# State-space items re-spaced over later products, a reordered list of products, and ScalarE shifts in a two-block layer on one core

## Chip, cores and metric

One core of one Trainium2 chip runs the whole program. The metric is device microseconds (us) of one execution. Engines: TensorE (PE; its weight loads are PEld), VectorE (DVE), ScalarE (ACT), GpSimd (POOL), and SyncE (SP), whose queue issues most of the DMAs.

## The reference, cut to what matters

The input is one sequence of 256 rows of width 1024 in float32. A first block (two layers: modulated norms, pooling, sparse attention, feed-forward) is followed by a second block, and the change lies in the second block alone, apart from one buffer count. What the second block computes:

```python
u = h @ w_in
z, xbc, dt_f_raw, dt_b_raw, q, k, v, gate_logits = split(u)
y_ssd = ssd_branch(z, xbc, dt_f_raw, dt_b_raw, ...) @ w_proj_ssd
y_att = attention_branch(q, k, v) @ w_proj_attn
gates = sigmoid(gate_logits + b_gate)
mix = (gates[0] * y_ssd + gates[1] * y_att) @ w_out
h = layer_norm(alpha * h + mix)
h = layer_norm(alpha * h + square(relu(h @ w_up)) @ w_down)
# ssd_branch, forward and backward in time, by chunks of 128 rows:
xbc = silu(conv5(xbc))                       # xs (32 heads of 64), B, C (4 groups of 128)
lmat = exp(a_cs[l] - a_cs[s])  for s <= l    # running sums of dt * a, head by head
y = (C B^T * lmat) @ (dt * x) + what comes from the other chunk + d_skip * x
y = y * silu(z); y = y * rsqrt(mean(y^2 over a group)) * norm_w
```

## The kernel before

Every weight matrix is loaded in chunks of 128 x 1024 (`Weights.load`, lines 129 to 147): a DMA on SP's queue into `wst`, a copy on ScalarE that rounds it to `wh` (line 140), and a subtraction on VectorE that leaves the rest in `wl` (line 141). Each product is then three matmuls (line 89 in the trace, the helper `mm`). In the second block at most `cap=4` chunks are alive at once.

`large2` (line 1540) is a generator that runs the products in the order of `ORDER2`: v0, qk0 to qk2, v1, B, C, then x0 x1 z0 x2 z1 x3 z2 z3, then the gates g2 g3, pa (attention projection), g0 g1, and ps (state-space projection). Each of these takes 8 steps, pa 4 and ps 32: x0 runs over steps 56 to 63, the next seven over 64 to 119, g2 over 120 to 127, g3 to 135, pa to 139, g0 to 147, g1 to 155, ps over 156 to 187. An x product ends in a convolution (`conv`, lines 1319 to 1332): per half of its columns two scalings on ScalarE, eight VectorE instructions on line 1330, a tanh on ScalarE (line 1331) and a product on VectorE (line 1332). A z product ends in `zgate` (lines 1343, 1344).

Between the steps a `Plan` (lines 326 to 358) emits other work. Each entry has a step from which it may run and names of what it needs. The state-space work is 16 items, one for each group g (of 4), chunk t (of 2) and half of the group's heads (sub, of 2). Item i is placed at a = ss0 + ds * i, with ss0=73 and ds=4.2: steps 73 to 136. Its parts:
- `ssd_r` at a-6: two row loads on SP's queue (line 1421) into R, forward and backward running sums spread over all partitions
- `ssd_g` at a-3.5: four ScalarE scalings and four VectorE instructions (lines 1431, 1433)
- `ssd_d` at a: per head a ScalarE shift of the backward plane `u` (line 1443) and a VectorE instruction that subtracts the forward sum from `E` and takes the minimum with `u` (line 1444), then one exp (line 1445) and one product (line 1446)
- `ssd_y` at a+3.5: matmuls; for the second half of a pair also the sums (lines 1461 to 1467, one of them on GpSimd)
- `ssd_norm` at a+8 for the second half: product with z, square on ScalarE, power on GpSimd, scaling (lines 1472 to 1477)

`ssd_fm` (line 1481) of a group turns its two normed tiles y by TensorE transposes, scales them (line 1489) and splits them into high and low parts (lines 103, 106), which `proj_ssd` multiplies. Its step is a + sf with sf=300, past the end of the list, so it is emitted only when `proj_ssd` asks for it: `plan.until(("fm", k // 4))` ahead of chunk k = 0, 4, 8 and 12.

Work tiles are of one kind, `t2` (128 x 512 float32), with `nt2=22` buffers for the whole program. What is emitted earlier has the higher priority; the framework's scheduler may still put a later instruction ahead of one that, by its own reckoning, is not ready.

Of the kernel before, what the change touches and what calls it, by code (L numbers as in the profile page):

```python
# [11 lines left out]
AF = mybir.ActivationFunctionType  # L12
OP = mybir.AluOpType
# [11 lines left out]
ALPHA = 2.0 ** 0.25  # L25

SZ = 1024
TU = dict(nst=5, tabc=2, nw=9, nt2=22, raw=1, krest=2, qrest=4, pool2=1, c2=3, c3=1, c4=1, ln=3, uv='uv', pre=[1], nv=5, nv1=0, nv0=0, u0=19.5, du=0.7, ub=2, uc=4, c0=32.5, dc=0.1, w0=36, dw=0.5, comp=22, pool=27, dpool=2, cmpa=32, cmpb=34, dcmp=2, e1=1, e0=1, pta=2, ahead=3, modp=3, rf=0.95, r0=0, r0b=2, r1=0.8, r1b=1.2, rs=14, raw_=4, qrest_=6, u0_=19.5, du_=1.0, comp_=22, pool_=26, cmpa_=31, cmpb_=35, nv_=0, nv0_=0, w0_=32, dw_=0.8, order2='v0 qk0 qk1 qk2 v1 B C x0 x1 z0 x2 z1 x3 z2 z3 g2 g3 pa g0 g1 ps', dts=8, dcd=30, par0=10, par1=40, d0=50, dd=2, db=3, dc2=5, ss0=73, ds=4.2, scb=5, sx=3, sr=6, sg=3.5, sy=3.5, sn=8, sf=300, mf0=5, modp1=99, rf1=0.5, pool2_=3, c3_=2, c4_=3, nv1_=2, dpool_=2, dcmp_=1, dc_=0.4, cap=4, ub_=2.5, c0_=32.5, pta_=4)
NST, NW = TU['nst'], TU['nw']
NT2, NT4, NS5 = TU['nt2'], 5, 20  # L30

ORDER2 = TU["order2"].split()

MODS = {("mix", 0): ((0, 2), (0, 3), (0, 4)), ("ff", 0): [(0, 5), (1, 1), (1, 0), (1, 2), (1, 3), (1, 4)][:TU["mf0"]],
        ("mix", 1): [(0, 5), (1, 1), (1, 0), (1, 2), (1, 3), (1, 4)][TU["mf0"]:], ("ff", 1): ((1, 5),)}
CONV2 = {"x0": 0, "x1": 4, "x2": 8, "x3": 12, "B": 16, "C": 20}
# [23 lines left out]
def tile_two_blocks(ctx: ExitStack, tc: tile.TileContext, I, out, stop=None, dbg=None):  # L62
    nc = tc.nc
    V, A, G, T = nc.vector, nc.scalar, nc.gpsimd, nc.tensor
# [10 lines left out]
    def bank(tag):  # L75
        return pp.tile([128, 512], FT, name=tag, tag=tag, bufs={"acc": 4, "st": 2, "tr": 1, "pv": 1}[tag])
# [8 lines left out]
    def s5(shape, name, dt=FT):  # L85
        return small.tile(shape, dt, name=name, tag="s5", bufs=NS5)

    def mm(o, l, r, start, stop=False):
        T.matmul(o, l, r, start=start, stop=stop, skip_group_check=True)  # L89

    def fl(a):
        return a.rearrange("p a b -> p (a b)")
# [17 lines left out]
    def C(n):  # L110
        a, w = CC[n]
        return cst[:, a:a + w]
# [363 lines left out]
    for l in range(DEPTH):  # L476
        wi, wo = kt_view(I["w_in"][l]), kt_view(I["w_out"][l])
        g = {}
        cols = {"u": (0, 512), "q": (512, 1024), "k": (1024, 1536), "v": (1536, 1816)}
        if l == 0:  # L480
            for k in range(0, 8, 2):
                for n in "qk":
                    W.specs.append(([wi[:, k:k + 2, cols[n][0]:cols[n][1]]], 2, 512))
        for n in "qk" + TU["uv"]:
            if l or n in "uv":
# [6 lines left out]
    g2 = {}  # L492
# [715 lines left out]
    av, dt_, wo_, ed, sums = (s5([128, 2, 64], n) for n in ("av", "dt_", "wo_", "ed", "sums"))  # L1208
# [24 lines left out]
    def chunk_decays():  # L1233


        b = bank("st")
        for t in range(2):
            mm(b[0:32, t * 128:(t + 1) * 128], av[:, t, 0:32], C("j_le_l"), t == 0, True)
            mm(b[32:64, t * 128:(t + 1) * 128], av[:, t, 32:64], C("j_lt_s"), t == 0, True)
        rows = small.tile([64, 2, 128], FT, name="rows")  # L1240
        A.activation(fl(rows)[0:32], b[0:32, :256], AF.Copy)
        A.activation(fl(rows)[32:64], b[32:64, :256], AF.Copy, scale=-1.0)
        nc.scalar.dma_start(rows_d.rearrange("t h l -> h t l"), rows)
        b = bank("st")
        for t in range(2):
            T.transpose(b[:, t * 64:(t + 1) * 64], rows[:, t], ident[:64, :64])
        bv = b[:, :128].rearrange("p (t h) -> p t h", t=2)
        V.tensor_copy(sums[:, :, 0:32], bv[:, :, 0:32])
        V.tensor_scalar(sums[:, :, 32:64], bv[:, :, 32:64], -1.0, None, op0=OP.mult)
        b = bank("tr")  # L1250
        mm(b[:, 0:32], C("s_lt_j"), av[:, 0, :32], True, True)
        mm(b[:, 32:64], C("j_lt_s"), av[:, 1, 32:], False, True)
        mm(b[:, 64:96], C("j_ge_l"), av[:, 0, 32:], False, True)
        mm(b[:, 96:128], C("j_le_l"), av[:, 1, :32], False, True)
        A.activation(fl(ed), b[:, :128], AF.Exp)
        for t in range(2):
            V.scalar_tensor_tensor(wo_[:, t, :32], fl(ed)[:, t * 32:t * 32 + 32], 0.5, dt_[:, t, t * 32:t * 32 + 32], op0=OP.mult, op1=OP.mult)
# [178 lines left out]
    def ssd_d(g, t, sub):  # L1436


        a0 = g * 8 + sub * 4
        E, u = ssd.pop(("R", g, t, sub))  # L1440
        for i in range(4):
            h = a0 + i
            A.activation(u[:, i], u[:, i], AF.Identity, bias=sums[:, t, 32 + h:33 + h])
            V.scalar_tensor_tensor(E[:, i], E[:, i], sums[:, t, h:h + 1], u[:, i], op0=OP.subtract, op1=OP.min)  # L1444
        A.activation(fl(E), fl(E), AF.Exp)
        V.tensor_tensor(E, E, ssd.pop(("G", g, t, sub)), op=OP.mult)  # L1446
        ssd["M", g, t, sub] = E
# [111 lines left out]
    plan = Plan()  # L1559
    plan.at(TU["dts"], steps, needs=("v0",), gives="steps")  # L1560
    plan.at(TU["dcd"], chunk_decays, needs=("steps",), gives="decays")
    for i in range(2):
        plan.at(TU["par%d" % i], parity, i, needs=(f"v{i}",), gives=f"par{i}")
    for i in range(8):
        e, j = i // 4, i % 4
        a = TU["d0"] + TU["dd"] * i
# [6 lines left out]
    for i, it in enumerate(items):  # L1573
        g, t, sub = it
        a = TU["ss0"] + TU["ds"] * i
        if it[1:] == (0, 0):
            plan.at(a - TU["scb"], ssd_cb, g, needs=("B", "C", "steps"), gives=("cb", g))
            for tt in range(2):
                plan.at(a - TU["sx"] + 2 * tt, ssd_x, g, tt, needs=(f"x{g}", "decays"), gives=("x", g, tt))
        plan.at(a - TU["sr"], ssd_r, *it, needs=("decays", prev and ("r",) + prev), gives=("r",) + it)  # L1580
        plan.at(a - TU["sg"], ssd_g, *it, needs=(("cb", g),), gives=("g",) + it)
        plan.at(a, ssd_d, *it, needs=(("r",) + it, ("g",) + it), gives=("d",) + it)
        plan.at(a + TU["sy"], ssd_y, *it, needs=(("d",) + it, ("x", g, 0), ("x", g, 1), prev and ("y",) + prev), gives=("y",) + it)
        if sub:
            plan.at(a + TU["sn"], ssd_norm, g, t, needs=(("y",) + it, f"z{g}{t}"), gives=("n", g, t))
            if t:
                plan.at(a + TU["sf"], ssd_fm, g, needs=(("n", g, 0), ("n", g, 1)), gives=("fm", g))
        prev = it
    plan.got.add(None)
    plan.run(large2())  # L1590
# [170 lines left out]
```

## Time and profile before

| | us |
|---|---|
| median of 3 runs (1280.6 to 1288.57) | 1282.55 |
| the profiled execution: its time | 1284.53 |
| the profiled execution: its span | 1282.4 |
| TensorE busy | 1179.8 (92%) |
| VectorE busy | 895.9 (70%) |
| ScalarE busy | 642.4 (50%) |
| GpSimd busy | 237.0 (18%) |

The span runs from the first to the last instruction; the execution's time is 2.1 us longer. Times in the rows below count from the span's start. Matmuls are pipelined and their ends are modelled, so a busy TensorE may still be waiting for little things. An instruction's duration on VectorE and ScalarE is longer than the distance to the start of the next, because neighbours overlap a little.

### The profile page before, as it was taken

The page shows a single profiled execution, that of the slowest core. Times are in us where ns is not written, and L with a number is a line of the kernel's source. Part 1 is how long each engine was busy: PE and PEld are TensorE (multiplying, and loading weights), DVE is VectorE, ACT ScalarE, POOL GpSimd, SP SyncE. Part 2 cuts the span into 40 slices and gives each one's busy share as a digit, 9 for nine tenths or more (in the row PEclk, how much of TensorE's full clock was granted, in tenths as well). Part 3 has the DMA queues.
Part 4 walks back from the last instruction along what each step waited for, and adds up shares of the span by engine and source line. Part 5 has one row for each costly group of instructions (what it writes and reads, how often), then busy time and mean ns, then how long its engine had stood idle before and what let it go on. Part 6 is the DMA issues. An engine that isn't in the chain of part 4 may idle for free.

```text
span 1282.4 us, 19159 instructions
## 1 busy us (share of the span) xinstructions
PE 1179.8 (92%) x7188; PEld 1037.6 (81%) x7188; DVE 895.9 (70%) x1446; ACT 642.4 (50%) x1070; POOL 237.0 (18%) x233
## 2 busy tenths in 40 slices
PE   4878898999898899999999999988898899999997
PEld 3656776899787788789998999977688888799896
DVE  5777798887758768764545738799999557754544
ACT  4346355444535554744543545485675434544440
POOL 3553322112315101210100000011112001210101
PEclk9788889999999999999999999989899899999999
DMA  7855667889878534566663663564466753666640
GB/s 268 284 174 180 230 214 230 292 297 330 289 218 266 189 99 119 190 207 192 181 193 101 216 200 102 195 174 139 135 191 189 258 151 98 226 210 188 183 145 33
DMA packets 101780, 249.18 MB, mean 194 GB/s; under 512 B 9780, under 2 KB 15028, under 8 KB 101688
## 3 DMA queue, kind: packets, MB, share of 16 engines
q1 hardware_dynamic: 100904, 247.12, 60.6%
q8 instruction: 56, 0.92, 0.3%
q10 hardware_dynamic: 784, 0.85, 0.2%
q14 instruction: 36, 0.29, 0.1%
HBM read 246.03 MB, written 1.11 MB: 193 GB/s over the span
## 4 chain that ended last, share of the span: by engine, by line
PE 38%; issue 10%; DVE 8%; ACT 1%; POOL 1%; DMA 0%; DVEq 0%; POOLq 0%; ACTq 0%
PE acc L89 23%; PE st L89 12%; DVE wl L141 2%; DVE R L1444 1%; DVE cv L1330 1%; PE pv L89 1%; DVE G L1433 1%; DVE R L1446 1%; ACT wh L140 1%; POOL yss L119 0%; DVE ytmp L1465 0%; DMA wst<-in_w_up_dram 0%; PE tr L89 0%; POOL fr L380 0%; DVE yg L1477 0%
## 5 line engine op out<-in xcount | busy, mean ns | idle before, releaser
L141 DVE TENSOR_TENSOR wl<-wst,wh 128x1024 fp32r<-128x1024 f32 (+3 forms) x340 | 418.6, 1244 | 164.7 <-ACT wh L140 163.7
L140 ACT ACTIVATE wh<-wst 128x1024 fp32r<-128x1024 f32 (+3 forms) x340 | 352.1, 1048 | 314.2 <-PE acc L89 98.1
L89 PE MATMUL st<-hh,wh 128*128 128x256 f32 x576 | 163.0, 283 | 0.0
L89 PE MATMUL st<-hl,wh 128*128 128x256 f32 x576 | 163.0, 283 | 0.0
L89 PE MATMUL st<-hh,wl 128*128 128x256 f32 x576 | 163.0, 283 | 0.0
L89 PE MATMUL acc<-wh,frl 128*128 128x512 f32 x384 | 151.8, 395 | 2.4 <-DVE frl L381 2.3
L89 PE MATMUL acc<-wl,frh 128*128 128x512 f32 x384 | 150.6, 392 | 0.0
L89 PE MATMUL acc<-wh,frh 128*128 128x512 f32 x384 | 150.3, 391 | 0.0
L380 POOL TENSOR_TENSOR fr<-fr 128x512 f32<-128x512 f32 x48 | 64.7, 1349 | 384.7 <-ACT frh L379 376.4
L89 PE MATMUL acc<-hh,wl 128*128 128x256 f32 x416 | 122.1, 294 | 1.4 <-DVE wl L141 1.4
L89 PE MATMUL acc<-hl,wh 128*128 128x256 f32 x416 | 119.0, 286 | 0.0
L89 PE MATMUL acc<-hh,wh 128*128 128x256 f32 x416 | 118.7, 285 | 0.0
L89 PEld LDWEIGHTS st<-hh,wl 128*128 128x128 f32 x576 | 110.5, 192 | 0.7
L89 PEld LDWEIGHTS st<-hl,wh 128*128 128x128 f32 x576 | 110.5, 192 | 0.7
L89 PEld LDWEIGHTS st<-hh,wh 128*128 128x128 f32 x576 | 110.5, 192 | 0.0
L89 PE MATMUL acc<-wl,hh 128*128 128x512 f32 (+3 forms) x224 | 90.6, 405 | 13.1 <-DVE wl L141 13.1
L89 PE MATMUL acc<-wh,hl 128*128 128x512 f32 (+3 forms) x224 | 90.2, 413 | 12.4 <-ACT wh L140 9.9
L548 DVE SCALAR_TENSOR_TENSOR macc<-wst,cact,macc 128x1024 f32<-128x1024 f32 x70 | 91.7, 1311 | 7.5 <-DMA wst<-in_w_mod_dram 3.9
L89 PE MATMUL acc<-wh,hh 128*128 128x512 f32 (+3 forms) x224 | 90.6, 405 | 0.0
L89 PEld LDWEIGHTS acc<-wh,frl 128*128 128x128 f32 x384 | 72.6, 189 | 19.6 <-DVE frl L381 5.4
L89 PEld LDWEIGHTS acc<-wh,frh 128*128 128x128 f32 x384 | 72.5, 189 | 15.5
L89 PEld LDWEIGHTS acc<-wl,frh 128*128 128x128 f32 x384 | 72.5, 189 | 14.0
(328 smaller groups left out, 2289.6 us busy)
## 6 DMA issues: line engine op xcount, KB each, us to landing
wst<-in_w_ff_dram SPq DMA_DIRECT2D x128, 512.0 KB, 4.4
wst<-in_w_mod_dram SPq DMA_DIRECT2D x96, 512.0 KB, 4.6
wst<-in_w_in_dram SPq DMA_DIRECT2D x92, 512.0 KB, 4.8
wst<-in_w_up_dram SPq DMA_DIRECT2D x32, 512.0 KB, 4.3
wst<-in_w_down_dram SPq DMA_DIRECT2D x32, 512.0 KB, 4.3
wst<-in_w_out_dram SPq DMA_DIRECT2D x24, 512.0 KB, 4.2
R<-rows SPq DMA_DIRECT2D x32, 256.0 KB, 5.4
wst<-in_w_proj_ssd_dram SPq DMA_DIRECT2D x16, 512.0 KB, 4.7
```

Source lines behind the costliest of these rows:

```text
L89: T.matmul(o, l, r, start=start, stop=stop, skip_group_check=True)
L140: A.activation(h[:, :kc * n], st[:, :kc * n], AF.Copy)
L141: V.tensor_tensor(l[:, :kc * n], st[:, :kc * n], h[:, :kc * n], op=OP.subtract)
L380: G.tensor_tensor(r, r, r, op=OP.mult)
L548: V.scalar_tensor_tensor(acc, st, cact[:, k:k + 1], acc, op0=OP.mult, op1=OP.add)
L1330: V.scalar_tensor_tensor(v[:, a:e], u[:, a + j - 2:e + j - 2], w[:, j:j + 1], v[:, a:e], op0=OP.mult, op1=OP.add)
L1433: V.scalar_tensor_tensor(gm[:, i], cl, dt_[:, t, 32 + a0 + i:33 + a0 + i], gm[:, i], op0=OP.mult, op1=OP.add)
L1444: V.scalar_tensor_tensor(E[:, i], E[:, i], sums[:, t, h:h + 1], u[:, i], op0=OP.subtract, op1=OP.min)
L1446: V.tensor_tensor(E, E, ssd.pop(("G", g, t, sub)), op=OP.mult)
```

## The change

- `nt2` goes from 22 to 24.
- In `order2` the x and z products take turns: x0 z0 x1 z1 x2 z2 x3 z3.
- The items go to a = 70 + 5.6 * i: steps 70 to 154 (ss0=70, ds=5.6).
- `ssd_fm` of group g gets the step fm0 + dfm * g = 148 + 9 * g (148, 157, 166, 175); `sf` is gone.
- The column form of the running sums, `sums`, is negated for the forward half too, in one instruction in place of two.
- In `ssd_d` ScalarE adds the negated sum to the forward plane as well, and the four fused VectorE instructions of an item become one minimum over 128 x 512.

```diff
-TU = dict(nst=5, tabc=2, nw=9, nt2=22,
...
-order2='v0 qk0 qk1 qk2 v1 B C x0 x1 z0 x2 z1 x3 z2 z3 g2 g3 pa g0 g1 ps', dts=8,
...
-ss0=73, ds=4.2, scb=5, sx=3, sr=6, sg=3.5, sy=3.5, sn=8, sf=300,
+TU = dict(nst=5, tabc=2, nw=9, nt2=24,
...
+order2='v0 qk0 qk1 qk2 v1 B C x0 z0 x1 z1 x2 z2 x3 z3 g2 g3 pa g0 g1 ps', fm0=148, dfm=9, dts=8,
...
+ss0=70, ds=5.6, scb=5, sx=3, sr=6, sg=3.5, sy=3.5, sn=8,
...
-        V.tensor_copy(sums[:, :, 0:32], bv[:, :, 0:32])
-        V.tensor_scalar(sums[:, :, 32:64], bv[:, :, 32:64], -1.0, None, op0=OP.mult)
+        V.tensor_scalar(sums, bv, -1.0, None, op0=OP.mult)
...
         for i in range(4):
             h = a0 + i
+            A.activation(E[:, i], E[:, i], AF.Identity, bias=sums[:, t, h:h + 1])
             A.activation(u[:, i], u[:, i], AF.Identity, bias=sums[:, t, 32 + h:33 + h])
-            V.scalar_tensor_tensor(E[:, i], E[:, i], sums[:, t, h:h + 1], u[:, i], op0=OP.subtract, op1=OP.min)
+        V.tensor_tensor(E, E, u, op=OP.min)
         A.activation(fl(E), fl(E), AF.Exp)
...
-                plan.at(a + TU["sf"], ssd_fm, g, needs=(("n", g, 0), ("n", g, 1)), gives=("fm", g))
+                plan.at(TU["fm0"] + TU["dfm"] * g, ssd_fm, g, needs=(("n", g, 0), ("n", g, 1)), gives=("fm", g))
```

## Rows read from the trace of the kernel before

**Rows 1.** The page: busy time of each engine over the whole span.
```profile
PE 1179.8 (92%) x7188; PEld 1037.6 (81%) x7188; DVE 895.9 (70%) x1446; ACT 642.4 (50%) x1070; POOL 237.0 (18%) x233
```
**Rows 2.** Busy time by stretch: length, PE, PEld, DVE, ACT, POOL, PE clock, DMA share, GB/s.
```profile
830.00:993.00 163.00, 142.36 (x883) 123.48 (x882) 153.76 (x310) 112.06 (x235) 27.90 (x24) 0.93 0.57 165
993.00:1007.00 14.00, 14.00 (x120) 14.00 (x118) 9.84 (x9) 8.11 (x12) 0.00 (x0) 1.00 0.91 327
1007.00:1017.00 10.00, 6.58 (x35) 6.14 (x34) 6.49 (x13) 4.67 (x12) 0.00 (x0) 0.66 0.79 275
1017.00:1038.00 21.00, 21.00 (x178) 21.00 (x177) 8.58 (x7) 7.52 (x8) 0.00 (x0) 1.00 0.49 154
1038.00:1046.00 8.00, 5.24 (x43) 4.77 (x42) 6.49 (x13) 4.47 (x10) 0.00 (x0) 1.00 0.43 131
...
808.80:1007.00 198.20, 177.56 (x1159) 157.59 (x1158) 181.53 (x360) 129.30 (x269) 27.90 (x24) 0.94 0.59 175
```
**Rows 3.** The chain that ended last, 879 to 898: start, us, what.
```profile
883.37 1.22 DVE wl L141
...
886.92 1.05 DVE R L1444 x4
...
889.75 0.60 DVE R L1446
...
894.08 0.60 DVE yg L1461
894.68 0.60 DVE ytmp L1465
895.28 2.08 DVE R L1444 x4
```
**Rows 4.** Waits, 808 to 1007: who waited for whom, us in total, times, longest.
```profile
ACT R L1443 <- DMA R<-rows: 11.5, 8, 7.3
...
PE acc L89 <- ACT wh L140: 9.9, 2, 5.8
...
PE pv L89 <- DVE R L1446: 6.8, 8, 2.7
```
**Rows 5.** ScalarE in order of time: start, us, instruction, count, idle before it.
```profile
825.78 1.28 ACT L1443 ACTIVATE R<-R,sums 128x128 f32<-128x128 f32 x4 [7.27 <-DMA R<-rows]
826.97 1.26 ACT L1431 ACTIVATE G<-cbu,dt__6387 128x128 f32<-128x128 f32 x4
...
912.93 1.15 ACT L1331 ACTIVATE page<-cv 128x512 f32<-128x512 f32 x2 [2.56 <-DVE cv L1330]
913.98 4.83 ACT L140 ACTIVATE wh<-wst 128x1024 fp32r<-128x1024 f32 x5
```
**Rows 6.** TensorE in order of time, at the third convolution and in ps.
```profile
908.64 0.60 PE L1487 MATMUL st<-cst,yg 128*128 128x128 f32 x4
915.08 1.74 PE L89 MATMUL acc<-wh,hl 128*128 128x512 f32 x3 [5.83 <-ACT wh L140]
...
1007.00 0.60 PE L1487 MATMUL tr<-cst,yg 128*128 128x128 f32 x4
1008.38 0.65 PE L1487 MATMUL tr<-cst,yg 128*128 128x128 f32 x4 [0.79 <-DVE yw L1489]
1011.67 1.09 PE L1487 MATMUL st<-cst,yg 128*128 128x128 f32 x4 [2.63 <-DVE yw L1489]
```
**Rows 7.** VectorE in order of time: two transposed groups, ahead of ps's first matmuls.
```profile
1010.84 0.69 DVE L1489 TENSOR_TENSOR yw<-st,par 128x512 f32<-128x512 f32 x1
1011.44 0.68 DVE L1489 TENSOR_TENSOR yw<-tr,par 128x512 f32<-128x512 f32 x1
1012.04 1.42 DVE L106 TENSOR_TENSOR yl<-yw,yh 128x256 fp32r<-128x256 f32 x4
1013.37 0.69 DVE L1489 TENSOR_TENSOR yw<-st,par 128x512 f32<-128x512 f32 x1
```
**Rows 8.** SP's queue, whole span: what its DMAs waited for, us, times, longest.
```profile
SPq L135 <- DVE wl L141: 696.2, 262, 17.6
...
SPq L1421 <- DVE G L1433: 4.3, 1, 4.3
...
SPq L1421 <- ACT zs L1474: 2.8, 2, 1.6
...
SPq L702 <- DMA wst<-in_w_in_dram: 2.3, 2, 1.4
```

More of the change, by code (lines that the diff above doesn't have):

```diff
@@ L27 @@
 SZ = 1024
-TU = dict(nst=5, tabc=2, nw=9, nt2=22, raw=1, krest=2, qrest=4, pool2=1, c2=3, c3=1, c4=1, ln=3, uv='uv', pre=[1], nv=5, nv1=0, nv0=0, u0=19.5, du=0.7, ub=2, uc=4, c0=32.5, dc=0.1, w0=36, dw=0.5, comp=22, pool=27, dpool=2, cmpa=32, cmpb=34, dcmp=2, e1=1, e0=1, pta=2, ahead=3, modp=3, rf=0.95, r0=0, r0b=2, r1=0.8, r1b=1.2, rs=14, raw_=4, qrest_=6, u0_=19.5, du_=1.0, comp_=22, pool_=26, cmpa_=31, cmpb_=35, nv_=0, nv0_=0, w0_=32, dw_=0.8, order2='v0 qk0 qk1 qk2 v1 B C x0 x1 z0 x2 z1 x3 z2 z3 g2 g3 pa g0 g1 ps', dts=8, dcd=30, par0=10, par1=40, d0=50, dd=2, db=3, dc2=5, ss0=73, ds=4.2, scb=5, sx=3, sr=6, sg=3.5, sy=3.5, sn=8, sf=300, mf0=5, modp1=99, rf1=0.5, pool2_=3, c3_=2, c4_=3, nv1_=2, dpool_=2, dcmp_=1, dc_=0.4, cap=4, ub_=2.5, c0_=32.5, pta_=4)
+TU = dict(nst=5, tabc=2, nw=9, nt2=24, raw=1, krest=2, qrest=4, pool2=1, c2=3, c3=1, c4=1, ln=3, uv='uv', pre=[1], nv=5, nv1=0, nv0=0, u0=19.5, du=0.7, ub=2, uc=4, c0=32.5, dc=0.1, w0=36, dw=0.5, comp=22, pool=27, dpool=2, cmpa=32, cmpb=34, dcmp=2, e1=1, e0=1, pta=2, ahead=3, modp=3, rf=0.95, r0=0, r0b=2, r1=0.8, r1b=1.2, rs=14, raw_=4, qrest_=6, u0_=19.5, du_=1.0, comp_=22, pool_=26, cmpa_=31, cmpb_=35, nv_=0, nv0_=0, w0_=32, dw_=0.8, order2='v0 qk0 qk1 qk2 v1 B C x0 z0 x1 z1 x2 z2 x3 z3 g2 g3 pa g0 g1 ps', fm0=148, dfm=9, dts=8, dcd=30, par0=10, par1=40, d0=50, dd=2, db=3, dc2=5, ss0=70, ds=5.6, scb=5, sx=3, sr=6, sg=3.5, sy=3.5, sn=8, mf0=5, modp1=99, rf1=0.5, pool2_=3, c3_=2, c4_=3, nv1_=2, dpool_=2, dcmp_=1, dc_=0.4, cap=4, ub_=2.5, c0_=32.5, pta_=4)
 NST, NW = TU['nst'], TU['nw']
```

## Prediction

> **What bounds the kernel now.** I read the page first, then the chain that ended last, then busy time by stretch, then waits and timelines where the change touches. Over the whole span TensorE is busy 92% and VectorE 70% [rows 1], which suggests that work on VectorE is free. The stretch in question says otherwise. I cut it at 808.8, where ScalarE takes the first columns of x0 (step 63), and at 1007.0, where the last matmul of g1 gives way to ps's first transposes (step 156). In these 198.2 us VectorE is busy 181.5, TensorE 177.6 at a clock share of 0.94, ScalarE 129.3. From 830 to 993 VectorE is busy 153.8 of 163.0, that is 94.3%, and TensorE only 142.4, at 0.93; from 993 on VectorE has 9.8 of 14.0 and TensorE is full [rows 2]. So the items keep VectorE saturated until 993, the weight halves on line 141 come late, TensorE starves, and only then runs at its own pace. The chain says the same: around 890 it goes through VectorE instruction after instruction [rows 3].
>
> Two further losses matter. At 915.08 TensorE had waited 5.83 us for `wh`, because the copies of line 140 stood on ScalarE behind line 1331, which itself waited for the convolution on VectorE [rows 5, 6]. And ps begins with the transposes of `ssd_fm`: TensorE waits for VectorE's `yw` and for the halves [rows 6]. From 1017 to 1038 it does 178 matmuls in 21.0 us, 0.118 each. By that price the 35 from 1007 to 1017 need 4.1 of the 10.0 us (loss 5.9, with the clock share at 0.66), and the 43 from 1038 to 1046 need 5.1 of 8.0 (loss 2.9): together 8.8 us [rows 2]. The groups come in two bunches, not four, since the scheduler moves some of it ahead: the first transposes on bank `st` run at 908.64 [rows 6]. A step of the plan is thus a priority, not a time.
>
> **The change, part by part.**
>
> *Negated sums.* One VectorE instruction less, once, some sixty steps before it is used: nothing.
>
> *Minimum in one instruction.* VectorE loses 64 fused instructions: four take 1.05 us on the chain, or 2.08 right after `ytmp`, when GpSimd is adding [rows 3]. It gains 16 minima over 128 x 512; not in the trace, but the product of line 1446 has the same shape and operands and takes 0.60 [rows 3]. 16 x (1.05 - 0.60) = 7.2 us less work. The slow variant would make it 16 x 1.48 = 23.7, but it is a wait for GpSimd that the next instruction with two SBUF operands can inherit, so I take 7.2; 0 is the other end.
>
> *Shifts on ScalarE.* 64 more of a kind it already does. Four start at 825.78 and the next instruction at 826.97: 0.30 each, 19.0 us in all [rows 5]. ScalarE then has 129.3 + 19.0 = 148.3 in the stretch, against 198.2 - 129.3 = 68.9 us of idle time that covers it [rows 2]. I cost it at nothing on the path. If the cover fails, what is late is the `wh` copy queued behind the shifts, then `wl`, then TensorE: up to 19.0. An item also needs both R planes ahead of its first shift now; the wait on row loads is 11.5 us in 8 places [rows 4] and could at worst double.
>
> A rule of the Trainium skill speaks against this part: "ScalarE: Activation LUTs", Rules for kernel authors, wants add, multiply and the like on VectorE and not on ScalarE. By engine time the rows agree with it, since 19.0 us are paid for 7.2. By it the change would lose; that is the slower rival below.
>
> *Spreading the items.* Sixteen items over 84 steps in place of 63. Nothing is removed. Work moves from the saturated part into g0, g1 and the start of ps, where VectorE has room. Past step 156 go the last pair's sums and norm (0.60 + 0.60 [rows 3], and about as much for lines 1472 and 1477): 2.3 us. Into the stretch comes `ssd_fm` of group 0, two `yw` at 0.60 and four halves in 1.33: 2.5 us [rows 7]. VectorE's work in the stretch becomes 181.5 - 7.2 - 2.3 + 2.5 = 174.5.
>
> How fast can that be done? At a full VectorE, 174.5 us, 23.7 less than now. At the share it held while it had a backlog, 94.3%, 174.5 / 0.943 = 185.0: 13.2 less. At the share of the whole stretch now, 181.5 / 198.2 = 91.6%, 190.5: 7.7 less. I take the middle one. The convolutions still saturate VectorE up to x3, and from g2 on TensorE and VectorE are about equally loaded, so neither will be full all the time.
>
> *x and z in turn.* After x0 the same six products fill the next 48 steps; x1, x2 and x3 each come 8 steps later. Convolutions no longer stand two in a row at x0 x1, but the wait of `wh` behind line 1331 stays possible for each x. The items still find their x: group 3 needs x3 at step 134.2, and it is there at 112. Nothing either way.
>
> *`ssd_fm` early.* Steps 148, 157, 166 and 175 stand 8, 7, 6 and 5 steps ahead of use at 156, 164, 172 and 180. A step of ps is about 1.4 us (12 matmuls at 0.118 [rows 2]), so each group has 7 us or more, against a chain of transposes, `yw` and halves that took 1007.00 to about 1013 for two groups [rows 6, 7]. The 8.8 us go. Group 3 needs the last norm (step 162), thirteen steps before. VectorE is busy 8.6 of 21.0 in ps, ScalarE 7.5 [rows 2]: that covers both. Low bound: the tiles are short and the first group stays late, half of 5.9 remaining, about 6 us gained.
>
> *Two more `t2` buffers.* The items of a pair and the finished y live longer, `ssd_fm` takes four tiles a group earlier, and I count some 24 in use at step 150, so the two buffers are used up by the change itself. In the first block loads into such tiles hardly wait on SP (2.3 us for the convolution weights of line 702), and the row loads of line 1421 wait 4.3 and 2.8 in their largest rows [rows 8]: nothing to gain, and I allow 3 us either way for a schedule that comes out otherwise.
>
> **The sum.** -13.2 - 8.8 = -22.0 against the profiled execution's own 1284.5: 1262.5. The median lies 2.0 below that execution, so 1260.5; I say 1260.
>
> **The rivals.**
>
> *VectorE or TensorE runs full.* Fewer gaps bring the clock back from 0.94 as well. TensorE's idle time in the stretch is 198.2 - 177.6 = 20.6, VectorE's floor gives 23.7 [rows 2]. With the 8.8 that is 29 to 32 less: 1250 to 1253. For it: the idle time is all waits for VectorE and ScalarE. Against: line 141 depends on line 140, and both engines do their work in order.
>
> *Only the transposes' share comes.* ScalarE, at 148.3, delays the copies about as often as VectorE did, or VectorE drops to 91% once TensorE holds it back. Then at most 7.7 of the stretch and 6 to 8.8 of ps, down to 3 in all: 1268 to 1280. For it: TensorE already waits 9.9 us for `wh` in two places [rows 4]. Against: ScalarE has the idle time.
>
> *Slower: ScalarE becomes what is waited for.* One mechanism: the forward shifts stand ahead of weight copies in ScalarE's order, all 19.0 us land on the path, with the second plane's row loads waited for as long as the first's (11.5 [rows 4]), and nothing of VectorE's saving is seen: 19.0 + 11.5 - 8.8 = +21.7, 1304. It decides once ScalarE's work plus its waits pass the stretch: 148.3 plus at least 50 of the present 68.9. Against: 20 or more of these are waits for weight loads and for TensorE, which shrink when ScalarE is late.
>
> **How the numbers follow.** Changes under 1%, 13 us, can hardly be told from none. The forecast, 1253 to 1268, has 0.56; the full-engine rival 0.17; the small-gain rival 0.20, a quarter of it still over 1% faster; the slower rival 0.07. Faster by over 1% means below 1269.7: 0.56 + 0.17 + 0.05, less a little for the sum's upper edge, 0.75; slower by over 1% 0.07; the rest 0.18. The range for 8 in 10 goes from 1246 (a full VectorE and 3 us of luck in the schedule) to 1277; the forecast's own is 1253 to 1268.
>
> **What would show it.** In the changed profile x0's end should come near 809 as before, and ps's first matmul near 994 in place of 1007. The stretch should show VectorE with about 174 busy, TensorE over 94% busy, ScalarE near 148. No drop of the clock share at the start of ps; line 1489's instructions spread over 980 to 1040, and ps's sixteen chunks in about 16 x 24 x 0.118 = 45 us. Line 1443 should have 64 more instructions beside it at 0.30 each. It is wrong if waits of TensorE for `wh` grow beyond 10 us, if row loads wait on SP for tiles, or if x0's end itself moves by more than 3 us.

## The result and the profile after

| | before | after |
|---|---|---|
| median, us | 1281.57 (4 runs) | 1266.59 (4 runs, 1263.57 to 1267.73) |
| ratio, 95% interval | 1 | 0.9872 (0.9827 to 0.9916) |
| span of the profiled execution, us | 1282.4 | 1264.3 |

The change makes the kernel 1.3% faster: 15.0 us by the medians, 16.4 by the ratio. The prediction was 1260 in a range from 1246 to 1277: the direction and the range hold, and a quarter to a third of the forecast gain of 22 us is missing. Of the two terms of the sum, the one for ps came out a little larger than forecast, and the one for the stretch ahead of ps less than half as large.

The page of the changed kernel, its busy times, answers [rows 1]:

```profile
PE 1176.0 (93%) x7188; PEld 1036.2 (82%) x7188; DVE 889.3 (70%) x1397; ACT 658.5 (52%) x1134; POOL 241.0 (19%) x233
```

VectorE loses 49 instructions (48 in `ssd_d`, one of the sums) and 6.6 us; ScalarE gains 64 and 16.1 us.

For all kernels I now cut at places that can be found in each: from the first ScalarE scaling of x0's convolution (line 1327 of before) to the first gate columns of g1 (line 1359), called the stretch; and from there to the last use of a gate in ps (line 1534), called ps. By that cut, busy time by stretch (length, PE, PEld, DVE, ACT, POOL, PE clock, DMA share, GB/s), first the two rows of before:

```profile
808.80:1006.50 197.70, 177.06 (x1154) 157.09 (x1154) 181.39 (x360) 128.80 (x268) 27.90 (x24) 0.94 0.59 174
1006.50:1066.10 59.60, 53.43 (x419) 52.34 (x418) 33.91 (x49) 24.76 (x39) 0.00 (x0) 0.94 0.51 165
```

and of the changed kernel:

```profile
806.80:998.40 191.60, 178.04 (x1170) 159.47 (x1169) 173.00 (x311) 145.69 (x333) 31.91 (x22) 0.95 0.59 180
998.40:1048.10 49.70, 48.86 (x400) 48.25 (x401) 34.69 (x49) 24.43 (x39) 2.61 (x2) 1.00 0.60 191
```

ps is 9.9 us shorter and the clock drop at its start is gone. The stretch is only 6.1 us shorter, though VectorE has 8.4 us less to do: its busy share fell from 91.7% to 90.3%. Another 2.0 us lie ahead of x0 (808.8 against 806.8). That says nothing: up to the first scaling of product B all kernels here have the same instructions in the same order, but for the one instruction of the sums, and that mark lies anywhere from 763.0 to 771.3 in their profiles. So lengths are compared, not places.

One place where the stretch loses time is its end. There the chain that ended last runs so (start, us, what):

```profile
990.94 5.64 DMA R<-rows
996.58 0.02 issue
996.60 0.69 ACT R L1443 x2
...
998.47 1.08 ACT sig L1358 x3
```

SP's queue in the same place (the eight weight loads wait for a free `wst` between them):

```profile
971.13 18.32 SPq L135 DMA_DIRECT2D wst<-in_w_proj_ssd_dram  x8
989.50 1.81 SPq L1420 DMA_DIRECT2D R<-rows  x2
```

and ScalarE and TensorE there, with the idle time before each:

```profile
994.75 0.69 ACT L1442 ACTIVATE R<-R,sums 128x128 f32<-128x128 f32 x2 [1.43 <-DMA R<-rows]
996.60 0.69 ACT L1443 ACTIVATE R<-R,sums 128x128 f32<-128x128 f32 x2 [1.15 <-DMA R<-rows]
...
998.37 1.17 ACT L1358 ACTIVATE sig<-acc,bgh 128x256 f32<-128x256 f32 x3
```
```profile
999.24 0.39 PE L89 MATMUL acc<-yh,wl 128*128 128x256 f32 x1 [2.02 <-ACT sig L1358]
```

The last item's row loads stand on SP behind eight weight loads of ps, which go out only as VectorE's line 141 frees `wst` (166.2 us of SP's waits from 807 to 1010, in 51 places). On ScalarE the gate columns of g1 stand behind the shifts that wait for the rows, and TensorE, which has begun ps at 994.95, waits 2.02 us for these columns.

### The profile page after: what moved, and what is told of

Read it like the earlier page. It is cut to its first block, busy times and chain, and to the rows that moved or that the text cites. A ratio compares the mean times of both kernels' runs of the same rounds, so it can differ in the third digit from the quotient of the medians.

```text
span 1264.3 us, 19132 instructions
## 1 busy us (share of the span) xinstructions
PE 1176.0 (93%) x7188; PEld 1036.2 (82%) x7188; DVE 889.3 (70%) x1397; ACT 658.5 (52%) x1134; POOL 241.0 (19%) x233
## 4 chain that ended last, share of the span: by engine, by line
PE 41%; DVE 6%; issue 6%; ACT 2%; DMA 2%; POOL 1%; SPq 0%; DVEq 0%; POOLq 0%; ACTq 0%
PE acc L89 25%; PE st L89 13%; DVE wl L141 2%; DVE cv L1329 1%; DMA R<-rows 1%; PE pv L89 1%; ACT wh L140 1%; PE tr L89 1%; POOL yg L1467 0%; DMA wst<-in_w_up_dram 0%; DVE G L1432 0%; ACT R L1443 0%; DVE R L1446 0%; POOL fr L380 0%; DMA wst<-in_w_in_dram 0%
```

## The experiments

From e1 on, the medians are of five rounds, and each ratio is to the kernel before, timed in the same rounds on the same chip. e1 to e4 ran together, e5 to e8 together, e9 to e12 together, each group on a chip of its own, where the kernel before had medians of 1282.5, 1285.7 and 1283.1; across groups the ratios are compared. The lengths of the stretch and of ps come from each kernel's one profile. The change and e7 are the same instructions in the same order on every engine, so the distance between their rows shows how well a number repeats.

| kernel | median | ratio to before (95%) | stretch | ps |
|---|---|---|---|---|
| before | 1281.6 | 1 | 197.7 | 59.6 |
| the change | 1266.6 | 0.9872 (0.9827 to 0.9916) | 191.6 | 49.7 |
| e1: before + early `ssd_fm` | 1271.6 | 0.9916 (0.9891 to 0.9942) | 202.4 | 49.7 |
| e9: before + ScalarE shift | 1268.6 | 0.9891 (0.9866 to 0.9915) | 186.1 | 58.7 |
| e11: before + spread items | 1278.8 | 0.9979 (0.9959 to 0.9999) | 189.6 | 64.7 |
| e12: before + early rows | 1285.5 | 1.0019 (0.9997 to 1.0040) | 200.8 | 62.4 |
| e2: change, late `ssd_fm` | 1277.4 | 0.9953 (0.9931 to 0.9975) | 187.1 | 64.2 |
| e3: change, shift on VectorE | 1269.8 | 0.9906 (0.9879 to 0.9933) | 195.2 | 53.9 |
| e4: change, no forward shift | 1264.3 | 0.9854 (0.9825 to 0.9884) | 185.8 | 56.4 |
| e5: change, packed items | 1262.6 | 0.9813 (0.9789 to 0.9837) | 189.5 | 49.7 |
| e6: change, old order | 1266.1 | 0.9837 (0.9816 to 0.9859) | 189.5 | 51.2 |
| e7: change, 22 buffers | 1266.1 | 0.9857 (0.9834 to 0.9879) | 192.4 | 49.7 |
| e8: change, early rows | 1260.0 | 0.9798 (0.9779 to 0.9818) | 182.8 | 51.3 |
| e10: change, packed, early rows | 1268.4 | 0.9870 (0.9847 to 0.9894) | 193.1 | 49.6 |

**The transposes: e1 and e2.** The edit of e1 on the kernel before; e2 is the reverse on the changed one.

```diff
-                plan.at(a + TU["sf"], ssd_fm, g, needs=(("n", g, 0), ("n", g, 1)), gives=("fm", g))
+                plan.at(TU["fm0"] + TU["dfm"] * g, ssd_fm, g, needs=(("n", g, 0), ("n", g, 1)), gives=("fm", g))
```

> The kernel before with one edit: ssd_fm gets the steps 148, 157, 166, 175 in place of being emitted when proj_ssd asks for it. Items, order, buffers and shifts stay as before. Theory A (each part pays by itself): the two stops of ps, 5.9 and 2.9 us, go and nothing else moves: 8 to 10 us less than before, about 1272. Rival B (the stops go only because the spread items leave VectorE and ScalarE free earlier): here VectorE is saturated until 993 and the transposes cannot come earlier, so 0 to 4 us less, about 1279.

> The changed kernel with ssd_fm emitted late again (a + 300, when proj_ssd asks). Theory A: the two stops at the start and in the middle of ps come back, 8 to 10 us more than the changed kernel, about 1276; the stretch from x0 to g1 keeps its length or gets shorter by the 2.5 us of VectorE's work for group 0. Rival B (the last pair, now running into ps, sets when ps can go on): the stop is worse than before, 12 us or more, since until() now also has to emit what is left of the last items: 1279 or more.

e1 takes 10.9 us off (1282.5 to 1271.6), and e2 gives 10.8 back (1266.6 to 1277.4; 10.4 by the ratios). Busy time in e1, stretch and ps:

```profile
805.50:1007.90 202.40, 181.27 (x1158) 161.64 (x1158) 183.85 (x366) 129.84 (x272) 27.71 (x24) 0.92 0.56 170
1007.90:1057.60 49.70, 49.70 (x415) 49.53 (x414) 31.36 (x43) 23.44 (x35) 0.00 (x0) 1.00 0.60 200
```

In ps TensorE is busy without a gap at full clock: 9.9 us less than before. VectorE's work in the stretch rises by the 2.5 us of group 0 (181.39 to 183.85). Theory A held by the medians: the transposes pay by themselves, and alone they bring two thirds of what the change brings. That nothing else moves is not seen: in this profile, of e1's slowest run (1275.7), the stretch is 4.7 us longer than before. In e2 the stop is back, and larger:

```profile
997.04 0.66 PE L1487 MATMUL tr<-cst,yg 128*128 128x128 f32 x4 [0.79 <-DVE ytmp L1465]
1000.62 1.11 PE L1487 MATMUL tr<-cst,yg 128*128 128x128 f32 x4 [2.92 <-DVE yw L1489]
1003.53 1.08 PE L1487 MATMUL st<-cst,yg 128*128 128x128 f32 x4 [1.80 <-DVE yw L1489]
```

ps takes 64.2 there, against 59.6 before. The first transposes wait for `ytmp`, which belongs to the last pair, so the place that rival B named is seen; its 12 us or more in the whole are not, and the stretch is 4.5 us shorter than with the early transposes.

**The shift: e9, e3, e4.** e9 puts the shift into the kernel before, with the negated sums that it needs; e3 takes it back in the changed one (the fused instruction with an add); e4 drops the added line alone. The part of e9's edit in `ssd_d`:

```diff
+            A.activation(E[:, i], E[:, i], AF.Identity, bias=sums[:, t, h:h + 1])
             A.activation(u[:, i], u[:, i], AF.Identity, bias=sums[:, t, 32 + h:33 + h])
-            V.scalar_tensor_tensor(E[:, i], E[:, i], sums[:, t, h:h + 1], u[:, i], op0=OP.subtract, op1=OP.min)
+        V.tensor_tensor(E, E, u, op=OP.min)
```

> The kernel before with the ScalarE shift, the negated sums and the one minimum, and nothing else of the change. Theory A (VectorE bounds the stretch until 993, and this is the one part that takes work off it): 7.2 us of VectorE work at a share of 0.94, so 5 to 8 us less than before. Rival B (only together with the spread items does it pay, since ScalarE's shifts come in bursts with packed items): 0 to 3 us less, or more than before.

> The changed kernel with the fused instruction back on VectorE (four of 128x128 per item that add the negated forward sum and take the minimum), so ScalarE loses the 64 added shifts and the minimum over 128x512 goes. Theory A (VectorE bounds the stretch, ScalarE has cover): 7.2 us of VectorE work come back at a share of 90 to 94%: 5 to 8 us more than the changed kernel, about 1273. Rival C (ScalarE's shifts ahead of weight copies cost more than they save, as the rule that wants such work on VectorE says): 4 us or more less than the changed kernel, 1262 or below. Rival D (both engines have slack once the items are spread): within 3 us, 1264 to 1270.

> The changed kernel without the 64 forward shifts on ScalarE, and with nothing in their place: the forward running sum is not subtracted, so this leaves out a part of the decay. It measures what the shifts cost by themselves. Theory A (covered by ScalarE's idle time): 0 to 3 us less than the changed kernel, 1264 to 1267. Rival C (they stand on the path): 8 us or more less, up to the 19.0 us they take, 1248 to 1258.

e9 is 14.5 us faster than before (1283.1 to 1268.6), twice what theory A wanted; rival B fell. Its stretch:

```profile
803.20:989.30 186.10, 171.95 (x1152) 153.14 (x1151) 173.13 (x312) 146.03 (x332) 31.47 (x24) 0.96 0.61 184
```

VectorE's work fell by 8.3 us and the stretch by 11.6. Two waits shrink beside the work. TensorE's wait for the finished plane was 6.8 us [rows 4], and the waits of before also have this line:

```profile
ACT R L1445 <- DVE R L1444: 6.4, 5, 2.8
```

The same two in e9:

```profile
PE pv L89 <- DVE R L1446: 2.8, 7, 0.7
ACT R L1445 <- DVE R L1444: 1.4, 3, 0.6
```

ScalarE's exp used to wait for four instructions of VectorE; now one, of 0.82 us in the mean, is enough. How much of the 11.6 us is work and how much is waits, no run separates. The waits for GpSimd do move on to other instructions, as the prediction held. VectorE's groups of before in the stretch, then of e9 (mean ns behind the busy time):

```profile
L1444 DVE SCALAR_TENSOR_TENSOR R<-R,sums 128x128 f32<-128x128 f32 x64 | 25.5, 454 | 0.0
L1433 DVE SCALAR_TENSOR_TENSOR G<-cbl,dt__6387,G 128x128 f32<-128x128 f32 x64 | 20.2, 359 | 0.0
```
```profile
L1432 DVE SCALAR_TENSOR_TENSOR G<-cbl,dt__6387,G 128x128 f32<-128x128 f32 x64 | 25.3, 439 | 0.0
L1444 DVE TENSOR_TENSOR R<-R 128x512 f32<-128x512 f32 x16 | 13.1, 820 | 0.0
```

The two lines together go from 45.7 to 38.4, 7.3 us; the line that builds G grows by 5.1 us without a change of its own. Without a GpSimd instruction beside it, the fused instruction takes 343 ns (48 of the 64), the minimum 682 (10 of 16) and an instruction of G 341 to 343; beside one, up to 1.4, 1.8 and 1.4 us. What the two lines lose in this way is 8.2 us before and 8.4 in e9: it only changed places.

In the changed kernel the shift is worth less. e3 is 3.2 us slower than the change by the medians and 4.4 by the ratios, with overlapping intervals; against e7 it is 6.3. So theory A and rival D are not told apart, and rival C fell. e4, which has no forward shift at all, is 2.3 us faster than the change (1264.3), within the noise: little of the 17 us that ScalarE does more in the stretch is on the path, and rival C's 8 us or more are not there. Its profile is no clean price of the shifts, since VectorE has 4.5 us less to do in the stretch and ps is 6.7 us longer (168.51 busy, 56.4 long).

**The spread: e11 and e5.**

```diff
-ss0=73, ds=4.2
+ss0=70, ds=5.6
```

> The kernel before with the items at 70 + 5.6 i and nothing else of the change. My prediction's step (the work moved into g0, g1 and ps shortens the stretch) wants 4 to 8 us less than before. Theory A (spreading as such is worth nothing, since TensorE has the items' matmuls to do in g0 and g1 instead): within 3 us of before. Rival B (the last pair then stands at the start of ps and ssd_fm waits for it): 3 us or more slower.

> The changed kernel with the items packed as before (ss0=73, ds=4.2), all else as changed. Theory A (what is left of the gain, about 5 us, comes from work moved into g0 and g1, where VectorE had room): the stretch from x0 to g1 is longer again and only the smaller VectorE work of the minimum stays: 3 to 6 us more than the changed kernel, 1270 to 1273. Rival B (spreading moves nothing, since VectorE's work is the same and the late items now stand in g1 and ps): within 2 us of the changed kernel, 1264 to 1268, or less.

Spreading alone brings 4.4 us by the medians (1283.1 to 1278.8) and 2.7 by the ratio, whose interval ends at 0.9999: theory A and my step's 4 to 8 us are not told apart, and rival B's slower kernel is not seen. The profile says why it is no more:

```profile
808.40:998.00 189.60, 172.28 (x1152) 155.13 (x1151) 174.50 (x352) 127.91 (x266) 29.34 (x22) 0.96 0.57 172
998.00:1062.70 64.70, 54.60 (x422) 52.55 (x422) 39.61 (x57) 25.66 (x42) 2.70 (x2) 0.92 0.55 178
```

The stretch does get 8.1 us shorter, as my step said. Of the 6.9 us of VectorE work that left it, 5.7 turn up in ps (33.9 to 39.6), where the late transposes wait for the last pair, as rival B said, and ps is 5.1 us longer:

```profile
1001.71 0.66 PE L1487 MATMUL tr<-cst,yg 128*128 128x128 f32 x4 [2.06 <-DVE ytmp L1465]
```

With the transposes early that return is avoided, and still the spread brings nothing in the change: packed items (e5) are 3.5 us faster than e7, the change's like in the same group (1262.6 against 1266.1; the intervals of the two ratios barely touch). Theory A of e5 fell, rival B's last words ("or less") held. What holds the spread back is seen with e8 and e10 below.

**Order and buffers: e6 and e7.** `order2` as before; `nt2=22`.

> The changed kernel with x0 x1 z0 x2 z1 x3 z2 z3 again. Theory A (the order is worth nothing, as predicted): within 2 us of the changed kernel, 1264 to 1268. Rival B (two convolutions in a row at x0 x1 are what stops TensorE longest): 4 us or more above it, 1270 or more.

> The changed kernel with 22 work buffers. Theory A (the two buffers are worth nothing): within 2 us of the changed kernel. Rival B (22 are too few for the spread items and the early transposes, so row loads and tiles wait): 4 us or more above it, with waits of SP or ScalarE for work tiles in the stretch.

Both give 1266.1, half a microsecond from the change, and theory A held in both. With 22 buffers the same instructions come in the same order, so e7 also serves as a second measurement of the change, beside e5 to e8. Both edits are worth nothing that can be told from noise.

**Rows earlier: e8, e10, e12.** `sr=6` becomes `sr=10`: in the changed kernel, in the changed kernel with packed items, and in the kernel before.

> The changed kernel with the row loads of every item ten steps ahead in place of six. In the changed kernel the last item's loads stood on SP's queue behind eight weight loads until 989.5, ScalarE waited for them at the head of its order until 996.6, and TensorE waited 2.2 us for the last gate columns behind them. Theory A (that wait is part of what the stretch gave back): it goes, and with it some of the other 7 us of waits for rows: 2 to 4 us less than the changed kernel, 1263 to 1265. Rival B (another wait takes its place, since VectorE is the bound): within 1.5 us.

> The changed kernel with the items packed as before (ss0=73, ds=4.2) and the row loads ten steps ahead. Theory A (row loads late on SP's queue were what the stretch lost, spreading as such is worth nothing): as fast as the spread items with early rows or up to 3 us faster, 20 to 29 us less than before. Rival B (packed items with early rows hold too many work tiles at once, or crowd VectorE again): 3 us or more slower than the spread items with early rows.

> The kernel before with the row loads ten steps ahead in place of six, nothing else. Theory A (ScalarE waiting for rows at the head of its order costs time in the kernel before too, 11.5 us of it in 8 places): 3 to 6 us less than before. Rival B (there VectorE is the bound and ScalarE's waits are covered; the wait costs only once the change has made both busy): within 2 us of before.

e8 has the lowest median, 1260.0, 6.1 us under its like in the same group (e7); the intervals of the ratios are apart (0.9779 to 0.9818 against 0.9834 to 0.9879). That is more than theory A wanted, and rival B fell. SP's queue in e8, then its stretch:

```profile
966.07 0.33 SPq L135 DMA_DIRECT2D wst<-in_w_proj_ssd_dram  x1
966.50 0.85 SPq L1420 DMA_DIRECT2D R<-rows  x2
972.30 25.44 SPq L135 DMA_DIRECT2D wst<-in_w_proj_ssd_dram  x13
```
```profile
808.70:991.50 182.80, 171.79 (x1146) 154.71 (x1146) 170.00 (x311) 144.99 (x330) 31.84 (x22) 0.96 0.61 183
```

The last rows go out at 966.5, ahead of the last thirteen weight loads, and ScalarE's waits for rows, 3.5 + 3.5 us in the change, are 0.5 and 0.8:

```profile
ACT R L1443 <- DMA R<-rows: 0.8, 2, 0.5
ACT R L1442 <- DMA R<-rows: 0.5, 2, 0.3
```

VectorE's share is 93.0%, with 3.0 us less work than in the change, and the stretch is 14.9 us shorter than before. The last 17.4 us of the stretch show it best; before, the change, e8:

```profile
989.10:1006.50 17.40, 17.40 (x147) 17.40 (x146) 13.16 (x14) 10.05 (x15) 1.40 (x1) 1.00 0.90 309
981.00:998.40 17.40, 16.23 (x138) 16.02 (x136) 13.39 (x21) 11.64 (x28) 3.67 (x2) 1.00 0.64 218
974.10:991.50 17.40, 17.40 (x149) 17.40 (x148) 16.61 (x27) 14.98 (x33) 3.54 (x2) 1.00 0.61 204
```

The spread was to bring work to VectorE there. In the change it does not (13.39 busy against 13.16), and TensorE has gaps; with the rows early it does (16.61), and TensorE is full.

With packed items (e10) early rows do harm: 0.9870 against 0.9813 of e5, with the intervals apart. Against e8 it is 0.9870 to 0.9798, so with early rows the spread is worth some 9 us; theory A of e10 fell and rival B held. Rival B's reason is seen on SP's queue: the row loads wait for work tiles 15.5 us in all, against 4.0 in e5 and 0.7 in e8. Their longest group in e10:

```profile
SPq L1420 <- PE pv L89: 4.8, 2, 3.7
```

Whether that is all of the harm, one profile of each does not settle. So the spread by itself (e7) and early rows by themselves (e10) are each slower than neither (e5), and both together (e8) are not: 1260.0 against 1262.6, with overlapping intervals.

In the kernel before, early rows do nothing (e12, 1.0019), which is rival B's number. Its reason, that the wait is covered there, is not tested: the wait does not go away. ScalarE waits 16.2 us for rows in e12, against 11.5 [rows 4], and SP's row loads wait 17.5 us for tiles, against 10.7 before.

```profile
ACT R L1443 <- DMA R<-rows: 16.2, 8, 6.7
```

## Why the prediction was right or wrong

- **What bounds the kernel.** Right for the kernel before. VectorE is full in the stretch, and the one edit that takes work off it (e9) has the largest gain of the parts alone, by its median; the interval of e1 overlaps it.
- **`ssd_fm` early, 8.8 us.** Right: 9.9 us in ps in e1 and in the change, 10.9 and 10.8 by the medians of e1 and e2.
- **VectorE's work in the stretch, 174.5.** Right: 173.0, and in its parts: 8.3 for 7.2 (e9), 2.5 for the 2.5 of group 0 (e1), 2.2 for the 2.3 of the last pair (e5 against the change). The choice of 7.2 over 23.7 was right for the reason given: the waits for GpSimd were inherited.
- **The share at which it is done, 94.3%.** The failed step: 90.3%. With it the stretch's term of 13.2 came out as 6.1; at 91.6%, the end that I did not take, it would have been 7.7. The 94.3% belong to 830 to 993, and the sum put them on the whole stretch, which has 91.6% in the kernel before: at 94.3% that kernel's own 181.5 us would take 192.5, not 198.2. So 5.7 of the 13.2 stood for spreading filling the last microseconds of the stretch. In the change this did not come, since the last rows wait on SP; not for tiles, as the prediction feared, but behind weight loads. With them early (e8) the end fills, the share is 93.0%, the highest of any kernel here together with e9, and the stretch is 8.8 us shorter than in the change, of which ps gives back 1.6. A lead of six steps does not count what stands ahead on the queue.
- **Which part earns it.** Wrong. I gave the shift 7.2 us of work and let spreading earn the rest. Alone the shift gives 11.6 in the stretch and the spread 8.1, of which ps takes 5.1 back (e11); in the change the spread costs about 3.5 (e5), and it pays only with early rows (e8 against e10). The parts do not add: alone they bring 28 to 30 us (10.9 + 14.5 + 4.4 by the medians), the change brings 15 to 16. That shift and spread relieve the same full VectorE is the likely reason, argued and not shown.
- **ScalarE's 19.0 us at nothing.** Right in cover and near in size: 16.9 more in the stretch, and no clear cost on the path (e4). TensorE's waits for `wh` fall from 9.9 us to 0.6, though not through the shift, which alone leaves 9.4 (e9). The rule of the Trainium skill ("ScalarE: Activation LUTs", Rules for kernel authors), which wants adds on VectorE, does not hold here: against it stands the gain of 14.5 us in e9. There VectorE is busy 91.7% of the stretch before the shift, ScalarE 65%. The slower rival, which followed it, was far off.
- **Order, buffers, sums: nothing.** Right for order and buffers (e6, e7); the sums were not run alone.
- **Luck.** The result lies at the upper edge of the forecast's own range, 1253 to 1268, but its stretch is that of the small-gain rival, which had VectorE drop to 91% and at most 7.7 us. That rival's own terms, 7.7 and 8.8, reach down to 1266. So the time alone could not choose between the two. The profile does: the ps term is the forecast's, the stretch term the rival's in size, though e8 shows late rows behind it and not, as that rival had it, TensorE holding VectorE back. The sign that failed says the same: TensorE was to be over 94% busy in the stretch, and is 92.9%.

TensorE's waits of the changed kernel in the stretch show what is left there, VectorE's halves after the convolutions first:

```profile
PE acc L89 <- DVE wl L141: 6.3, 3, 4.2
...
PE pv L89 <- DVE R L1446: 2.6, 3, 1.7
...
PE tr L89 <- DVE xo L1409: 2.4, 1, 2.4
...
PE acc L89 <- ACT wh L140: 0.6, 1, 0.6
```

## What to carry to other kernels

Edits need not add: here the parts alone sum to almost twice the whole, and two edits that each cost time by themselves in the changed kernel with packed items and late rows, the spread and the early rows, cost none together. Measure each alone, and then each as the one missing, before the sum is believed. A busy share read in the middle of a stretch does not hold for its ends unless the change brings work there, and then the loads for that work must be on the queue in time: count a load's lead against what stands ahead of it on the same DMA queue. An operation may go to the engine that is slower at it when the faster one is full: here 17 us on ScalarE bought 8 us on VectorE and shortened the stretch by 12. And when an edit meant to remove a wait changes nothing, look whether the wait is gone (e12) before it is called harmless.

## What the runs showed that was not expected

The waits for GpSimd are not tied to an instruction: when the fused instructions went, the untouched line that builds G rose from 359 to 439 ns in the mean (e9), and in the whole change the weight halves of line 141 rose from 1239 to 1302 ns while G fell to 351. And the first 770 us, the same instructions in the same order in every kernel but for the one of the sums, ended at places up to 8.3 us apart in fourteen profiles, half of what the whole change brings.
